# A joined set of edits in front of the state-space branch of a hybrid diffusion block, and two key units ahead of it

## The chip, the core and the metric

The kernel runs on one core of a Trainium2 chip. The metric is the device time of one execution in microseconds (us). The core has TensorE (PE in the profile; its weight loads are PEld), VectorE (DVE), ScalarE (ACT), GpSimd (POOL) and SyncE (SP), which here only issues DMAs. ACT issues DMAs as well, most of them stores. POOL issues a few.

## The reference, cut to what matters

One layer on 2048 latent tokens and 256 context tokens, width 1024. The input is normalised and modulated, projected once, and read by three branches: a 2-D Fourier mix, a bidirectional diagonal state-space scan (S5), and neighbourhood attention. The branches are gated, merged and projected; an MLP with squared ReLU follows.

```python
hx = modulate(rmsnorm(x, g_norm1[i]), sh1, sc1)
hc = modulate(rmsnorm(ctx, g_norm1[i]), mod_c[0], mod_c[1])
zx = hx @ w_in                       # 256 f | 256 u | 512 q | 512 k | 512 v | 3 x 1024 gates
zc_s5 = hc @ w_in[:, OFF_S5:OFF_Q]
zc_kv = hc @ w_in[:, OFF_K:OFF_G]
fa_x = fourier_mix(zx[..., :OFF_S5])
sb_x, sb_c = s5_branch(zx[..., OFF_S5:OFF_Q], zc_s5, ...)
nc_x = na_latent(qx, kx, vx, kc, vc, rpb)     # rpb: relative-position bias
out_x = gated_merge(fa_x, sb_x, nc_x, zx[..., OFF_G:], w_br_a, w_br_b, w_br_c, w_out)
x = x + gt1 * out_x
h2 = modulate(rmsnorm(x, g_norm2[i]), sh2, sc2)
x = x + gt2 * sqrelu_mlp(h2, w_ff1[i], w_ff2[i])
```

## The kernel before

Every product is made of three float32r products: each operand is split into a high part (rounded) and a low part (the rest), and `mm3` adds high by high, high by low and low by high (lines 179 to 181). A split is a copy on ACT for the high part and a subtraction on DVE or POOL for the low part (`splitw`, lines 169 to 175).

The projection is cut into units. A unit (`a_unit`, `gate`) takes 128 columns of `w_in`: `wunit` loads them on SP (tile `wraw`, two buffers, line 218), splits them into `whi` and `wlo` (two buffers each), and PE makes 24 products for each block of 512 tokens in PSUM tag `g`. ACT evicts to a tile `ev` (three buffers) and issues the store to DRAM. The kinds are f (Fourier), u (S5), q, k, v and gate. A q eviction also has a low part, made by DVE (line 325), and ACT issues the stores of both. The tokens are worked in two halves of 1024: `hx0`, then `hx1`, each 8 pairs of tiles.

A scheduler sets the order of the instructions on every engine and queue. It goes by readiness in its own model of time, and among ready instructions it takes the one that stands earlier in the program. Each engine and each queue then works strictly in that order. `issue_after(x)` puts DMAs behind x on their queue. Pools are stacks of memory, left and right; a pool opened after another was closed reuses its memory and waits for its last readers.

The order of the program: modulation and `hx0`; the S5 parameters (`s5_prep`, three steps, on DVE and POOL); u and f units of `hx0`; `hx1` (lines 392 to 396); the second part of the modulation weights, 64 loads `wm` of 256 KB on SP, each added by DVE (lines 400 to 430); the bias table (lines 433 to 447); the units of line 450 (k and v of `hx0`, u and f of `hx1`, q of `hx0`); S5; the late units of lines 467 to 469 (k, v, q of `hx1`, with `wlo` on POOL); the S5 gating; attention; 48 gate units; the merge and the MLP.

The bias table: `na_rpb` is transposed, mirrored by small copies on DVE and multiplied by a constant, giving `ro` of 120 x 128. Line 447 stores every row 64 times to `rpd` in DRAM, in pieces of 512 bytes. Attention reads it.

`hx0` is needed again for its gates, so `spill` stores it to DRAM, 1 MB for each of eight tile pairs. The Fourier stage's first table (`w1h`, `w1l`, 2 MB each) is copied from the constants to a DRAM tile `w1d` in eight transfers (line 461).

S5 (`s5`) has a drive (U, loaded by line 883, times L, loaded by line 899; lines 895 to 914), a scan on DVE alone (lines 945 to 978), and a readout. Its memory on the right side is that of `hx0`, so its loads begin when the last q unit of `hx0` is done. The Fourier branch (`fourier`) stands in the program between drive and scan. It has 16 table steps (line 532 on: load `zr` and the tables `fwh` and `fwl` from `w1d` on SP, products, copies to `ftA`). Then come `turn`, `tokens` and `channels`, whose PSUM results go through ACT twice, once as float32 (`Bf`, `Yf`) and once as the high part, and POOL subtracts (lines 561 and 578).

Of the kernel before, what the change touches and what calls it, by code (L numbers as in the profile page):

```python
# [94 lines left out]
def f32(t):  # L95
    return t.bitcast(F32)
# [3 lines left out]
def block_kernel(ctx: ExitStack, tc: tile.TileContext, I, out, C, stages=None, taps=None):  # L100
# [27 lines left out]
    gtd = dram.tile([2, D], F32, name="gtd")  # L128
    lmd = dram.tile([P, 512], F32, name="lmd")
    ld = dram.tile([8, P, 2, 256], F32, name="ld")  # L130
    w1d = dram.tile([2, P, 16, 256], F32, name="w1d")
    kmd = dram.tile([8, P, 256], F32, name="kmd")
    cd = dram.tile([8, P, 2, 2, P], F32, name="cd")
    x2d = dram.tile([2, KT, P, D], F32, name="x2d")
# [167 lines left out]
    def of_half(hx, half):  # L302
        return [(b * NB, NB, hx, half * HALF + b * NB) for b in range(2)]
# [54 lines left out]
    with pool("pa", side="right") as pa:  # L358
# [26 lines left out]
        for n in range(2):  # L385
            with tc.issue_after(lm):
                a_unit("u", n, of_half(hx0, 0) + [(0, CTX, hc, S)])
        next(prep5)
        next(prep5)
        for n in range(2):  # L390
            a_unit("f", n, of_half(hx0, 0))
        for _ in prep5:
            pass
        hst = ExitStack()
# [8 lines left out]
        for part in range(8):  # L403
# [16 lines left out]
            else:  # L420
# [7 lines left out]
                else:  # L428
                    nc.vector.tensor_tensor(a2[:, h], pt[:, 0:4], bm, op=OP.add)
                    nc.vector.scalar_tensor_tensor(a2[:, h], a2[:, h], 1.0, g2c[:, h], op0=OP.add, op1=OP.mult)  # L430


        rp = m2.tile([120, 31], F32, name="rp")
        nc.sync.dma_start(rp, I["na_rpb"].rearrange("l h a b -> (l h a) b"))
        pt = psum("t")
        nc.tensor.transpose(pt[0:31, 0:120], rp, ident[0:120, 0:120])
        rt = m2.tile([31, 8, 15], F32, name="rt")
        pv = pt[0:31, 0:120].rearrange("p (h a) -> p h a", h=8)
        for m in range(15):
            nc.vector.tensor_copy(rt[:, :, m], pv[:, :, 14 - m])  # L440
        rev = m2.tile([31, P], F32, name="rev")
        nc.sync.dma_start(rev, C["rev"])
        pt = psum("t")
        nc.tensor.matmul(pt[0:120, 0:P], rt.rearrange("p h a -> p (h a)"), rev, start=True, stop=True)
        ro = m2.tile([120, P], F32, name="ro")
        nc.vector.tensor_copy(ro, pt[0:120, 0:P])
        nc.sync.dma_start(rpd, ro[:, None, :].to_broadcast([120, 64, P]))
        m2s.close()

        for i, (kind, n) in enumerate([(c, n) for c in "kvufq" for n in range(2 if c in "uf" else 4)]):  # L450
            if kind in "uf":
                a_unit(kind, n, of_half(hx1, 1))
            else:
                a_unit(kind, n, of_half(hx0, 0) + ([] if kind == "q" else [(0, CTX, hc, S)]))
            with tc.issue_after(loads[-1]):
                if i < KT:
                    spill(hx0, i)
                elif i < 12:
                    r = slice((i % 4) * 32, (i % 4 + 1) * 32)
                    for e, nm in enumerate(("w1h", "w1l")):  # L460
                        nc.sync.dma_start(w1d[e, r], C[nm][r])

    g = K()
    g.__dict__.update(locals())
    if "s5" in stages:
        s5(g)
    for kind in "kvq":
        for n in range(4):
            a_unit(kind, n, of_half(hx1, 1), "pool")

    with pool("gl", side="right") as gl:
        wr = gl.tile([P, 2, 256], F32, name="wgr")
# [41 lines left out]
def fourier(g, ft):  # L514
# [13 lines left out]
    for ch in range(2):  # L528
        A = ft.tile([P, 2, 10, P], F32, name="ftA")
        for jj in range(8):  # L530
            zr = ft.tile([P, 2, P], F32, name="zr", bufs=2)
            nc.sync.dma_start(zr, zd[:, 2 * jj:2 * jj + 2, ch * P:(ch + 1) * P])
            zh = ft.tile([P, 2, P], F32R, name="zh", bufs=2)
            zl = ft.tile([P, 2, P], F32R, name="zl", bufs=2)
            g.splitw(zr, zh, zl)
            wh = ft.tile([P, 2, 256], F32R, name="fwh", bufs=2)
            wl = ft.tile([P, 2, 256], F32R, name="fwl", bufs=2)
            nc.sync.dma_start(f32(wh), g.w1d[0, :, 2 * jj:2 * jj + 2])
            nc.sync.dma_start(f32(wl), g.w1d[1, :, 2 * jj:2 * jj + 2])
            pt = psum("s")  # L540
            for j in range(2):
                mm3(pt[:, j * 256:(j + 1) * 256], zh[:, j], zl[:, j], wh[:, j], wl[:, j], True, True)
            for c in range(2):
                o = A[:, c].rearrange("p k (j i) -> p j k i", i=8)[:, 2 * jj:2 * jj + 2]
                i_ = pt.rearrange("p (j c k i) -> p c j k i", j=2, c=2, i=8)[:, c]
                for j in range(2):
                    nc.scalar.activation(o[:, j], i_[:, j, 0:10], AF.Copy)
# [3 lines left out]
        def turn(n):  # L551
# [3 lines left out]
            Bh = ft.tile([P, 2, 2, P], F32R, name="ftBh", bufs=2)  # L555
            Bl = ft.tile([P, 2, 2, P], F32R, name="ftBl", bufs=2)
            o = pt.rearrange("p (k c h) -> p k c h", k=2, c=2)
            Bf = ft.tile([P, 2, 2, P], F32, name="Bf")
            nc.scalar.activation(Bf, o, AF.Copy)
            nc.scalar.activation(Bh, o, AF.Copy)  # L560
            nc.gpsimd.tensor_tensor(Bl, Bf, f32(Bh), op=OP.subtract)
            B[n] = Bh, Bl

        def tokens(n):
# [7 lines left out]
            v = pt.rearrange("p (a c k) -> p a c k", a=2, c=2)  # L572
            Yh = ft.tile([P, 2, 2, P], F32R, name="Yh", bufs=2)
            Yl = ft.tile([P, 2, 2, P], F32R, name="Yl", bufs=2)
            Yf = ft.tile([P, 2, 2, P], F32, name="Yf")
            nc.scalar.activation(Yf, v, AF.Copy)
            nc.scalar.activation(Yh, v, AF.Copy)
            nc.gpsimd.tensor_tensor(Yl, Yf, f32(Yh), op=OP.subtract)
            Y[n] = Yh, Yl

        def channels(n):
# [1075 lines left out]
```

## Time and profile before

| what | us |
|---|---|
| median of 3 timed runs (lowest to highest) | 3142.71 (3140.58 to 3143.83) |
| the profiled execution | 3140.54 |
| its span, first to last instruction | 3138.8 |
| PE busy | 3007.0 (96%) |
| DVE busy | 2169.6 (69%) |
| ACT busy | 1422.8 (45%) |
| POOL busy | 940.5 (30%) |

All times inside the profile count from the first instruction of the span. "Busy" is the union of an engine's instructions. PE being busy does not mean that it is at full speed: the column PEclk gives the granted clock as a share of full. A name such as `ps_g<-hxh,whi` says what is written and what is read, without buffer numbers.

### The profile page before, as it was taken

Reading aid. Unit: us, or ns where it says so; the run is one execution under the profiler, and the core shown is the slowest. Engines: PE = TensorE matmul, PEld = TensorE weight load, DVE = VectorE, ACT = ScalarE, POOL = GpSimd, SP = SyncE. Lnnn points to the kernel's source line nnn. Section 1 sums busy time; section 2 is a strip of 40 time slices with the busy share of each in tenths; the row PEclk is TensorE's granted clock in tenths of the full one; section 3 lists DMA queues with packets and bytes.
Section 4 is the critical chain, followed back from the end, with each engine's and each line's share of the span. In section 5 each row is a group of like instructions: output and inputs, shape, how many; then the busy total and the mean of one; then the engine's idle time right before and its main releaser. Section 6 shows DMA issues by size and latency. Waiting matters only on the chain.

```text
span 3138.8 us, 40745 instructions
## 1 busy us (share of the span) xinstructions
PE 3007.0 (96%) x13974; PEld 2436.9 (78%) x13974; DVE 2169.6 (69%) x3654; ACT 1422.8 (45%) x2557; POOL 940.5 (30%) x865
## 2 busy tenths in 40 slices
PE   7999886899999999999999999999989999999998
PEld 4788675788788778887877788888867878878886
DVE  6534458984788888883748554777988475557788
ACT  4242143363566566653216555543432365555333
POOL 0520015301466655551511322311134022223111
PEclk9999988999999999999999999999999999999999
DMA  6669964456443633327533443845466334457442
GB/s 214 185 200 253 239 161 115 141 158 191 128 116 116 221 104 112 108 75 218 190 122 121 168 148 122 297 149 158 136 177 236 121 128 150 142 181 248 151 146 83
DMA packets 438213, 504.52 MB, mean 161 GB/s; under 512 B 95807, under 2 KB 281294, under 8 KB 437622
## 3 DMA queue, kind: packets, MB, share of 16 engines
q1 hardware_dynamic: 320646, 361.92, 38.2%
q10 hardware_dynamic: 116784, 139.09, 13.2%
q8 instruction: 110, 1.80, 0.2%
q0 software_dynamic: 576, 0.92, 0.1%
q14 instruction: 97, 0.79, 0.1%
HBM read 349.90 MB, written 156.11 MB: 161 GB/s over the span
## 4 chain that ended last, share of the span: by engine, by line
PE 65%; DVE 10%; DMA 5%; issue 1%; ACT 1%; SPq 1%; POOL 0%; ACTq 0%; DVEq 0%; POOLq 0%
PE ps_g L180 7%; PE ps_g L179 7%; PE ps_g L181 7%; PE ps_s L179 7%; PE ps_s L181 7%; PE ps_s L180 7%; PE ps_t L181 4%; PE ps_t L180 4%; PE ps_t L179 4%; PE ps_s L1110 3%; PE ps_o L1163 2%; PE ps_o L1162 2%; PE ps_o L1166 1%; DMA pgT<-rid 1%; DMA pgR<-in_w_out_dram 1%
## 5 line engine op out<-in xcount | busy, mean ns | idle before, releaser
L179 PE MATMUL ps_g<-hxh,whi 128*128 128x512 f32 x1024 | 407.1, 398 | 12.8 <-ACT ev L355 6.5
L180 PE MATMUL ps_g<-hxl,whi 128*128 128x512 f32 x1024 | 406.0, 396 | 0.0
L181 PE MATMUL ps_g<-hxh,wlo 128*128 128x512 f32 x1024 | 405.9, 397 | 0.0
L1160 POOL TENSOR_TENSOR pl<-st,ph 128x512 fp32r<-128x512 f32 (+7 forms) x256 | 270.4, 1071 | 165.6 <-ACT ph L1158 153.7
L1501 ACT ACTIVATE pgB<-pgB 128x1024 fp32r<-128x1024 f32 x112 | 118.8, 1061 | 303.6 <-PE ps_o L180 144.9
L179 PEld LDWEIGHTS ps_g<-hxh,whi 128*128 128x128 f32 x1024 | 195.0, 191 | 54.2 <-DVE ev L325 7.9
L180 PEld LDWEIGHTS ps_g<-hxl,whi 128*128 128x128 f32 x1024 | 195.0, 190 | 38.4 <-issue 0.5
L181 PEld LDWEIGHTS ps_g<-hxh,wlo 128*128 128x128 f32 x1024 | 195.1, 191 | 37.8
L1502 DVE TENSOR_TENSOR pgB<-pgB,pgB 128x1024 fp32r<-128x1024 f32 x112 | 148.5, 1327 | 89.0 <-ACT pgB L1501 88.9
L1353 DVE TENSOR_TENSOR pgW<-pgB,pgW 128x512 fp32r<-128x512 f32 x128 | 93.3, 733 | 142.3 <-ACT pgW L1352 142.3
L1132 DVE TENSOR_TENSOR mx<-mx,st 128x384 f32<-128x384 f32 (+2 forms) x224 | 184.5, 824 | 4.0
L180 PE MATMUL ps_s<-pgA,pgB 128*128 128x512 f32 x464 | 181.1, 390 | 0.0
L179 PE MATMUL ps_s<-pgA,pgB 128*128 128x512 f32 x464 | 181.1, 390 | 0.0
L181 PE MATMUL ps_s<-pgA,pgB 128*128 128x512 f32 x464 | 180.9, 390 | 0.0
L1390 POOL TENSOR_TENSOR pgR<-pgT 128x512 f32<-128x512 f32 x32 | 44.6, 1392 | 390.8 <-ACT pgT L1380 390.8
L1151 ACT ACTIVATE st<-st 128x512 f32<-128x512 f32 (+7 forms) x288 | 129.2, 494 | 66.2 <-DVE st L1150 56.6
L1537 POOL TENSOR_TENSOR pgA<-pgA,pgA 128x1024 f32<-128x1024 f32 x16 | 52.5, 3282 | 336.9 <-DMA pgA<-in_w_ff_dram 312.9
L1158 ACT ACTIVATE ph<-st 128x512 fp32r<-128x512 f32 (+7 forms) x288 | 135.7, 497 | 36.6 <-PE ps_o L1163 22.1
L180 PE MATMUL ps_g<-pgA,pgB 128*128 128x512 f32 x352 | 137.7, 391 | 1.3 <-DVE pgA L175 1.3
L179 PE MATMUL ps_g<-pgA,pgB 128*128 128x512 f32 x352 | 137.7, 391 | 0.0
L1150 DVE TENSOR_TENSOR st<-st,ps_t 128x512 f32<-128x512 f32 (+7 forms) x288 | 132.1, 524 | 8.1 <-PE ps_t L1142 8.0
L181 PE MATMUL ps_g<-pgA,pgB 128*128 128x512 f32 x352 | 137.5, 392 | 0.0
(506 smaller groups left out, 8418.9 us busy)
## 6 DMA issues: line engine op xcount, KB each, us to landing
pgB<-hcd SPq DMA_DIRECT2D x112, 512.0 KB
wraw<-in_w_in_dram SPq DMA_DIRECT2D x80, 512.0 KB
pgX<-in_w_ff_dram SPq DMA_DIRECT2D x64, 512.0 KB
hcd<-pgR ACTq DMA_DIRECT2D x64, 512.0 KB
pgA<-in_w_ff_dram SPq DMA_DIRECT2D x64, 512.0 KB
gd<-ev ACTq DMA_DIRECT2D x96, 256.0 KB
hcd<-pgT ACTq DMA_DIRECT2D x96, 256.0 KB
pgX<-gd SPq DMA_DIRECT2D x42, 512.0 KB
```

Of the source, the lines that this page charges most:

```text
L179: nc.tensor.matmul(out_, lh, rh, start=first, stop=False, skip_group_check=more)
L180: nc.tensor.matmul(out_, lh, rl, start=False, stop=False, skip_group_check=more)
L181: nc.tensor.matmul(out_, ll, rh, start=False, stop=last, skip_group_check=more)
L1110: nc.tensor.matmul(o, kk[:, j * P:(j + 1) * P], qs[:, i, p0:p1], start=i == 0, stop=i == 1)
L1132: v.tensor_tensor(M[:, c0:c1], M[:, c0:c1], st[:, c0:c1], op=OP.max)
L1150: v.tensor_tensor(st[:, c0:c1], st[:, c0:c1], mb[:, c0:c1], op=OP.subtract)
L1151: nc.scalar.activation(st[:, c0:c1], st[:, c0:c1], AF.Exp)
L1158: nc.scalar.activation(ph[:, c0:c1], st[:, c0:c1], AF.Copy)
L1160: e.tensor_tensor(pl[:, c0:c1], st[:, c0:c1], f32(ph)[:, c0:c1], op=OP.subtract)
L1353: v.tensor_tensor(p[:, 1], self.srcs[q][j], f32(p)[:, 0], op=OP.subtract)
L1501: nc.scalar.activation(h, s, AF.Copy)
L1502: v.tensor_tensor(l, s, f32(h), op=OP.subtract)
```

## The change

- The copy of the Fourier tables to `w1d` is gone. The Fourier steps read them from the constants, by DMAs that POOL issues into the float32r tiles.
- The spills: pairs 0 to 3 go out behind the loads of the two u units of `hx0`, pairs 4 to 7 behind the first four units of line 450.
- The bias table moves from the end of the second modulation part to the f units of `hx0`. It has a pool of its own. A further copy holds each row eight times, so that the store has pieces of 4 KB; it is cut in two, one behind each f unit's load.
- In `turn` and `tokens` ACT makes the high part alone, and DVE subtracts it from PSUM directly.
- The first two late units (k 0 and k 1 of `hx1`) stand ahead of S5 in the program, the other ten behind it as before. All twelve have `wlo` on DVE.

```diff
-    w1d = dram.tile([2, P, 16, 256], F32, name="w1d")
...
             with tc.issue_after(lm):
                 a_unit("u", n, of_half(hx0, 0) + [(0, CTX, hc, S)])
+            for k in range(2 * n, 2 * n + 2):
+                with tc.issue_after(loads[-1]):
+                    spill(hx0, k)
         next(prep5)
         next(prep5)
-        for n in range(2):
-            a_unit("f", n, of_half(hx0, 0))
+        with pool("rpp") as rpp:
...
+            ro = rpp.tile([120, P], F32, name="ro")
+            nc.vector.tensor_copy(ro, pt[0:120, 0:P])
+            ro8 = rpp.tile([120, 8, P], F32, name="ro8")
+            nc.vector.tensor_copy(ro8, ro[:, None, :].to_broadcast([120, 8, P]))
+            for n in range(2):
+                a_unit("f", n, of_half(hx0, 0))
+                with tc.issue_after(loads[-1]):
+                    r = slice(n * 60, (n + 1) * 60)
+                    nc.sync.dma_start(rpd[r].rearrange("r (a b) c -> r a (b c)", b=8),
+                                      ro8[r, None].rearrange("r a b c -> r a (b c)").to_broadcast([60, 8, 8 * P]))
...
-        rp = m2.tile([120, 31], F32, name="rp")
...
-        nc.sync.dma_start(rpd, ro[:, None, :].to_broadcast([120, 64, P]))
         m2s.close()
...
-            with tc.issue_after(loads[-1]):
-                if i < KT:
-                    spill(hx0, i)
-                elif i < 12:
-                    r = slice((i % 4) * 32, (i % 4 + 1) * 32)
-                    for e, nm in enumerate(("w1h", "w1l")):
-                        nc.sync.dma_start(w1d[e, r], C[nm][r])
+            if i < 4:
+                with tc.issue_after(loads[-1]):
+                    spill(hx0, 4 + i)
...
+    late = [(kind, n) for kind in "kvq" for n in range(4)]
+    for kind, n in late[:2]:
+        a_unit(kind, n, of_half(hx1, 1))
     if "s5" in stages:
         s5(g)
-    for kind in "kvq":
-        for n in range(4):
-            a_unit(kind, n, of_half(hx1, 1), "pool")
+    for kind, n in late[2:]:
+        a_unit(kind, n, of_half(hx1, 1))
...
-            nc.sync.dma_start(f32(wh), g.w1d[0, :, 2 * jj:2 * jj + 2])
-            nc.sync.dma_start(f32(wl), g.w1d[1, :, 2 * jj:2 * jj + 2])
+            nc.gpsimd.dma_start(wh, C["w1h"][:, 2 * jj:2 * jj + 2])
+            nc.gpsimd.dma_start(wl, C["w1l"][:, 2 * jj:2 * jj + 2])
...
-            Bf = ft.tile([P, 2, 2, P], F32, name="Bf")
-            nc.scalar.activation(Bf, o, AF.Copy)
             nc.scalar.activation(Bh, o, AF.Copy)
-            nc.gpsimd.tensor_tensor(Bl, Bf, f32(Bh), op=OP.subtract)
+            nc.vector.tensor_tensor(Bl, o, f32(Bh), op=OP.subtract)
...
-            Yf = ft.tile([P, 2, 2, P], F32, name="Yf")
-            nc.scalar.activation(Yf, v, AF.Copy)
             nc.scalar.activation(Yh, v, AF.Copy)
-            nc.gpsimd.tensor_tensor(Yl, Yf, f32(Yh), op=OP.subtract)
+            nc.vector.tensor_tensor(Yl, v, f32(Yh), op=OP.subtract)
```

## Rows read from the trace of the kernel before

**Rows 1.** The page's slices: busy tenths of PE, 40 slices of 78.5 us.
```profile
PE   7999886899999999999999999999989999999998
```
**Rows 2.** Windows: length, busy us (xinstructions) of each engine, PEclk, DMA share, GB/s.
```profile
356.00:659.00 303.00, 241.14 (x1195) 202.28 (x1194) 232.84 (x709) 105.95 (x251) 86.47 (x35) 0.89 0.56 146
...
600.00:656.00 56.00, 49.99 (x280) 42.90 (x279) 52.93 (x181) 24.15 (x51) 16.33 (x10) 1.00 0.33 97
...
800.00:1430.00 630.00, 627.03 (x3162) 502.55 (x3161) 527.21 (x945) 379.75 (x829) 364.75 (x502) 1.00 0.41 121
1430.00:1488.00 58.00, 55.19 (x235) 44.61 (x234) 15.71 (x20) 15.45 (x24) 0.00 (x0) 0.97 0.87 256
```
**Rows 3.** Timeline of PE: start, us, what, [idle before <-releaser].
```profile
393.33 0.61 PE L179 MATMUL ps_s<-Uh,Lh 128*128 128x288 f32 x1 [14.01 <-ACT Lh L171]
...
434.25 0.61 PE L179 MATMUL ps_s<-Uh,Lh 128*128 128x288 f32 x1 [10.31 <-ACT Lh L171]
...
504.37 0.55 PE L179 MATMUL ps_s<-fwh,zh 128*128 128x256 f32 x1 [15.00 <-DMA fwh<-w1d]
...
550.07 0.58 PE L179 MATMUL ps_s<-ft_w2h,ftBh 128*128 128x256 f32 x1 [7.19 <-ACT fa L595]
```
**Rows 4.** Timeline of SP's queue, 358 to 432 us.
```profile
360.54 5.21 SPq L883 DMA_DIRECT2D U<-ud  x5
...
371.32 5.82 SPq L408 DMA_DIRECT2D wm<-in_w_mod_dram  x3
...
384.14 0.90 SPq L899 DMA_DIRECT2D L<-ld  x2
...
405.11 1.01 SPq L447 DMA_DIRECT2D rpd<-ro  x1
406.64 24.05 SPq L899 DMA_DIRECT2D L<-ld  x2
```
**Rows 5.** Timeline of DVE in the drive.
```profile
433.00 0.26 DVE L970 COPY rev<-lam 128x16 f32<-128x16 f32 x2 [14.31 <-DMA rpd<-ro]
```
**Rows 6.** Timeline of POOL, 455 to 480 us.
```profile
455.51 0.75 POOL L522 DMA_DIRECT2D ft_w2h<-const_w2h_dram  x1 [9.08 <-DVE q L947]
...
459.86 2.46 POOL L175 TENSOR_TENSOR wlo<-wraw,whi 128x1024 fp32r<-128x1024 f32 x1 [2.00 <-ACT whi L171]
476.11 22.73 POOL L175 TENSOR_TENSOR wlo<-wraw,whi 128x1024 fp32r<-128x1024 f32 x1 [13.79 <-ACT whi L171]
```
**Rows 7.** Timeline of DVE at the same time.
```profile
460.02 2.58 DVE L175 TENSOR_TENSOR zl<-zr,zh 128x256 fp32r<-128x256 f32 x1
```
**Rows 8.** Groups of DVE, 450 to 655 us.
```profile
L325 DVE SCALAR_TENSOR_TENSOR ev<-ps_g,ev 128x512 fp32r<-128x512 f32 x8 | 5.4, 678 | 0.0
L175 DVE TENSOR_TENSOR wlo<-wraw,whi 128x1024 fp32r<-128x1024 f32 x4 | 4.9, 1221 | 1.8 <-ACT whi L171 1.8
```
**Rows 9.** Timeline of SP's queue, two neighbours in its order.
```profile
484.06 0.37 SPq L532 DMA_DIRECT2D zr<-zd  x1
498.87 0.38 SPq L218 DMA_DIRECT2D wraw<-in_w_in_dram  x1
```
**Rows 10.** Timeline of ACT in the Fourier stage.
```profile
549.36 0.65 ACT L595 ACTIVATE fa<-ps_s 128x256 f32<-128x256 f32 x1 [11.29 <-DVE q L947]
```
**Rows 11.** Windows in the first 300 us, columns as in rows 2.
```profile
60.00:80.00 20.00, 19.00 (x98) 13.99 (x96) 12.66 (x39) 11.12 (x23) 0.55 (x1) 1.00 0.13 29
...
235.00:300.00 65.00, 63.19 (x309) 52.03 (x308) 30.23 (x48) 14.04 (x24) 0.00 (x0) 1.00 0.97 264
```
**Rows 12.** Groups of POOL, 340 to 655 us: xcount | busy, mean ns | idle before.
```profile
L175 POOL TENSOR_TENSOR wlo<-wraw,whi 128x1024 fp32r<-128x1024 f32 x12 | 54.9, 4571 | 244.5 <-ACT whi L171 133.0 <-DMA wm<-in_w_mod_dram 111.4
L578 POOL TENSOR_TENSOR Yl<-Yf,Yh 128x512 fp32r<-128x512 f32 x10 | 16.9, 1692 | 17.5 <-ACT Yh L577 13.4 <-issue 4.1
```
**Rows 13.** Timeline of ACT: the high part of a gate unit's weights.
```profile
628.06 1.06 ACT L171 ACTIVATE whi<-wraw 128x1024 fp32r<-128x1024 f32 x1
```
**Rows 14.** Timeline of DVE: the low part of the same weights.
```profile
639.60 1.22 DVE L175 TENSOR_TENSOR wlo<-wraw,whi 128x1024 fp32r<-128x1024 f32 x1
```

More of the change, by code (lines that the diff above doesn't have):

```diff
@@ L387, in block_kernel @@
                 a_unit("u", n, of_half(hx0, 0) + [(0, CTX, hc, S)])
+            for k in range(2 * n, 2 * n + 2):
+                with tc.issue_after(loads[-1]):
+                    spill(hx0, k)
         next(prep5)
         next(prep5)
-        for n in range(2):
-            a_unit("f", n, of_half(hx0, 0))
+        with pool("rpp") as rpp:
+            rp = rpp.tile([120, 31], F32, name="rp")
+            nc.sync.dma_start(rp, I["na_rpb"].rearrange("l h a b -> (l h a) b"))
+            pt = psum("t")
+            nc.tensor.transpose(pt[0:31, 0:120], rp, ident[0:120, 0:120])
+            rt = rpp.tile([31, 8, 15], F32, name="rt")
+            pv = pt[0:31, 0:120].rearrange("p (h a) -> p h a", h=8)
+            for m in range(15):
+                nc.vector.tensor_copy(rt[:, :, m], pv[:, :, 14 - m])
+            rev = rpp.tile([31, P], F32, name="rev")
+            nc.sync.dma_start(rev, C["rev"])
+            pt = psum("t")
+            nc.tensor.matmul(pt[0:120, 0:P], rt.rearrange("p h a -> p (h a)"), rev, start=True, stop=True)
+            ro = rpp.tile([120, P], F32, name="ro")
[8 more added lines that the diff above has]
+                                      ro8[r, None].rearrange("r a b c -> r a (b c)").to_broadcast([60, 8, 8 * P]))
         for _ in prep5:
@@ L430, in block_kernel @@
                     nc.vector.scalar_tensor_tensor(a2[:, h], a2[:, h], 1.0, g2c[:, h], op0=OP.add, op1=OP.mult)
-        rp = m2.tile([120, 31], F32, name="rp")
[L434 to L446, printed above, removed]
-        nc.sync.dma_start(rpd, ro[:, None, :].to_broadcast([120, 64, P]))
         m2s.close()
```

## The prediction

> **What bounds the kernel now.** I read the page first, then windows by stage, then the waits inside the one stage that stands out. In the page's forty slices (78.5 us each) PE is at nine tenths or more but for the first, one near 2300 us, the last, and the fifth to the eighth, 314 to 628 us, where it falls to six [rows 1]. The windows say how much that is: from 356 to 659 us PE is busy 241.1 of 303 us, so 61.9 us are idle, and the granted clock averages 0.89; from 800 to 1430 us, attention with gate units as fill, PE is busy 627 of 630 [rows 2]. What the change can win lies in these 303 us: the start of the state-space branch, the Fourier branch and the scan on DVE. What it can lose lies anywhere.
>
> Four waits make 46.5 of the 61.9 us: 14.01 us before 393.33, 10.31 before 434.25, 15.00 before 504.37, 7.19 before 550.07 [rows 3]. The other 15.4 us are waits of at most a few us each.
>
> The first wait (A) ends with the split of the branch's first matrix. SP shows why it is late: the loads of U are issued from 360.5 on, but between them stand loads of the modulation weights (wm), and the load of L leaves only at 384.14 [rows 4].
>
> The second (B) is the bias table. Its store to rpd is issued at 405.11, and the next load on SP, the L that the drive needs, holds SP from 406.64 for 24.05 us [rows 4]. DVE stands too: a copy into a buffer that the store still reads starts at 433.00 after 14.31 us of idleness, released by that store [rows 5]. So one transfer stops two engines.
>
> The third (C) begins on POOL. A weight subtraction (wlo) that takes it 2.46 us at 459.86 takes 22.73 us at 476.11 [rows 6], amid the scan's back-to-back DVE instructions. The reverse happens too: at 460.02 DVE spends 2.58 us on a subtraction of 256 columns, while POOL's 2.46 us run [rows 7], though 1024 columns cost DVE 1.22 us otherwise [rows 8]. Both engines read two operands from SBUF, and they block each other. SP's next weight load waits for that wlo: nothing is issued between 484.06 and 498.87 [rows 9], and the Fourier tables queued behind it come late for PE at 504.37.
>
> The fourth (D) is ACT, held for 11.29 us in its own order until DVE, late against the order it was given, delivered a q eviction that ACT had to store [rows 10].
>
> **The change part by part.** *Bias table early, 4 KB rows.* The store leaves the drive. It no longer stands ahead of L on SP, and no scan buffer waits for it. B goes from 10.31 to between 0 and 3 us; I take 1, since the next L can still be late. What it costs at its new place: the small transposes and copies, one new copy of 120x1024 (nearest row 1.22 us on DVE [rows 8]) and the two stores, during the f units. SP is in order: if DVE delivers the copy late, the weight loads behind the store wait. I bound this by 0 and 6 us on PE and take 2.
>
> *Spills.* Eight pairs, 1 MB a pair, spread over the k and v units; now four pairs go out with the u units and four with the k units. From 60 to 80 us DMA is busy 0.13 [rows 11], so the first have room. Behind them on SP stand the weights of f: 0 to 4 us, I take 1.
>
> *The Fourier table's copy in DRAM goes.* Eight transfers of 512 KB leave SP; some of them lie in 235 to 300 us, where DMA is at 0.97 but PE is busy 63.2 of 65 us [rows 11]. So nothing comes directly. But the wm loads share SP and DMA with them, and wm is what delays L in A. I let A fall from 14.0 to between 3 and 14 us and take 7.
>
> *Two key units ahead of the branch.* PE already fills the time before A with late units; ahead in the order they can't come later, which protects A and gives nothing of its own: 0, bounds plus and minus 3.
>
> *wlo of the twelve late units, and Bl and Yl, from POOL to DVE.* POOL loses 54.9 us of wlo and 16.9 us of Yl [rows 12], as many Bl, and with them the blocked 22.73 us. DVE gains 12 x 1.22 = 14.6 us, and 20 subtractions that read PSUM, priced at the 0.68 us of the nearest row (128x512, one operand in PSUM), 13.6 us [rows 8]: 28 us in all. It gets back what POOL blocked: 12 x 2.46 + 20 x 1.69 = 63 us at most, nothing at least; DVE is busy 233 of 303 us [rows 2], so some three quarters of that fell on a busy DVE, and not all on an instruction with two SBUF operands. I take 25, under half. DVE's load is then about unchanged, and it is less late. ACT loses the 20 copies Bf and Yf, off the path. The new cover to watch: PSUM banks are held until DVE has read them.
>
> *Fourier tables from POOL's queue.* 32 loads leave SP, which no longer holds them behind a weight load. C's 15.0 us go to between 0 and 30 (the block twice over); I take 4. POOL's queue holds nothing else there. The trace has four such loads, issued from 455.51 amid the scan, 0.75 us for the first, and the POOL subtraction after them starts at 459.86 [rows 6]: they weren't stuck.
>
> By the Trainium skill, "SBUF — State Buffer", "SBUF: two separate sides", a DMA issued from GpSimd needs descriptors that GpSimd writes, and DVE in a two-port mode locks it out; "Who interferes with whom" adds that tensor_tensor takes only the read side, by inference. By the first sentence alone this edit walks into the trap that it means to leave; by the second it doesn't. The first row of [rows 6] fits the second. What the first would give is the second rival.
>
> *D and the small waits*, 7.2 and 15.4 us: many of them come from a late DVE. Between 5 and 23; I take 8.
>
> **The sum.** Idle in the stretch: 7 + 1 + 4 + 8 = 20 instead of 61.9, so 42 us. The clock: 0.89 over 303 us is about 67 us at the lower of its two levels (1.2 of 2.4 GHz), some half of it in the waits themselves; work at that level loses half its time, 2 to 33 us by how the two overlap, and I take 16. With a third of the idleness left, a third of this is left: 11 gained. The front costs 3. Total 42 + 11 - 3 = 50 us. A second way to the same: 241 us busy less 16 is 225 us of work at full clock; from 600 to 656 us, where gate units already have their wlo on DVE beside the scan, PE is busy 50.0 of 56 at clock 1.00 [rows 2]; 225 / 0.893 = 252 us, 51 less than 303.
>
> Does it reach the end? Behind this stretch PE is full, fed by gate units, and 58 us of gates alone follow attention [rows 2]. What is won earlier shortens that tail. The profiled execution took 3140.5 us (span 3138.8 and 1.7 around it), 2.2 under the median of 3142.7 and as fast as the fastest timed run. 3140.5 - 50 = 3090.5; on the median's footing 3093.
>
> **The rivals.** *DVE starves the weights (slower).* The late units' wlo now queues behind the scan. A gate unit's whi ends at 629.12 and its wlo starts on DVE at 639.60, 10.5 us later [rows 13, 14]; the q eviction of D was as late. With two buffers one unit's products cover it: 48 x 0.235 us (55.19 us for 235 products in the tail [rows 2]) = 11.3 us. Up to a lag of 10 us it is hidden; above, each of ten units pays the excess. The gain of 50 is gone at 5 us more each, a lag of 15; at 16 to 18 the time is 3093 + 60 to 80, so 3153 to 3173, with the upper part unlikely. For: DVE is busy 52.9 of 56 us from 600 to 656 us [rows 2]. Against: the same window, with gates' wlo on DVE, has PE at clock 1.00.
>
> *POOL's descriptors starve.* If the 32 loads are stuck in the scan's dense phases as wlo was for 20 us, PE pays a wait like C's 15 us once or twice: 3108 to 3123. For: the 22.73 us. Against: the four loads of [rows 6].
>
> *Given back.* The stretch shortens, but the gates taken forward are missing later: attention alone has DVE busy 527 of 630 [rows 2], and if the fill runs out before its end, or the loads behind attention lose the cover of the 58 us, up to all 50 come back: 3125 to 3148. It decides once the fill taken forward exceeds 58 us, which my sum does not.
>
> **How the numbers follow.** Forecast 0.60, 3093, own range 3064 (all waits and the slow clock gone, 79 us) to 3118. Starving descriptors 0.13. Given back 0.11. Starving weights 0.14. The other 0.02 is a front that costs tens of us. A change under 0.2% (6 us) is what a measurement of this kernel can't tell from none. Faster: 0.60 + 0.13 + 0.04 of the given back = 0.77. Same: 0.06 of the given back and 0.02 of a mild starving of weights, 0.08. Slower: the rest, 0.15. The range leaves out the starving weights and the top of the given back: 3064 to 3138.
>
> **What would show it.** B: no instruction on SP of more than a few us in the drive, no DVE idleness ended by rpd. C: no POOL subtraction in the Fourier stage, and first products of a table step not ended by its load. DVE: fewer instructions far above their group's usual length, and wlo starting within 10 us of whi. The tail of gates behind attention should be shorter or the whole should be earlier by the same amount. I am wrong if products of late units wait for wlo on DVE, if table loads land 15 us after their issue, or if the first 356 us grow by over 10.

## The result and the profile after

The changed kernel takes 3109.64 us (median of 4 runs, 3104.31 to 3111.11) against 3142.47 us (3140.58 to 3143.83) of the kernel before on the same chip: a ratio of 0.9893, 95% interval 0.9876 to 0.991. That is 33 us less, where 50 were forecast. The profiled execution took 3111.11 us, its span is 3109.3 us, against 3138.8 us before.

Where the 29.5 us between the two spans come from is read best from windows on either side of 375 us, just before the drive of the state-space branch. The columns are those of [rows 2]. First the kernel before:

```profile
0.00:375.00 375.00, 350.38 (x1754) 277.15 (x1755) 185.28 (x460) 122.68 (x215) 74.45 (x56) 0.97 0.75 218
375.00:700.00 325.00, 263.80 (x1350) 224.12 (x1349) 259.35 (x763) 133.38 (x307) 81.82 (x34) 0.89 0.55 150
```

and the changed kernel:

```profile
0.00:375.00 375.00, 334.65 (x1652) 263.94 (x1653) 189.05 (x478) 118.66 (x209) 66.34 (x53) 0.93 0.72 210
375.00:700.00 325.00, 308.15 (x1611) 263.48 (x1610) 263.47 (x799) 143.15 (x316) 19.40 (x36) 0.98 0.59 160
```

Two things happened. In the second stretch PE's idle time fell from 61.2 us (325 - 263.80) to 16.85, and the granted clock rose from 0.89 to 0.98. In the first, where the forecast put a cost of 3 us, the idle time rose from 24.6 to 40.4 us and the clock fell from 0.97 to 0.93.

For sums that take idle time and clock together I use one measure below, the **lost time** at a point of a trace: the time since the start less the time that the matmuls begun by then take without a stall (each shape at the 20th percentile of its distance to the next one, the same values for all kernels). Up to 375 us it went from 64.7 to 88.1 us, a loss of 23.4. From 375 to 700 us it went from 89.0 to 33.5 us, a gain of 55.5. Everything behind 700 us gave back 2.6 us. 55.5 - 23.4 - 2.6 = 29.5 us, the difference of the spans.

The waits of PE in the second stretch are short now (what waited, what it waited for: sum, times, longest):

```profile
PE ps_s L178 <- ACT Lh L170: 5.9, 1, 5.9
PE ps_g L178 <- DVE ev L324: 4.2, 4, 2.1
PE ps_s L180 <- DVE zl L174: 2.9, 2, 2.3
PE ps_s L180 <- DVE ftBl L565: 2.1, 1, 2.1
```

Of the four waits in [rows 3], A is 5.9 us long, and B, C and D are gone. In the first stretch a new one is longer than any of them. These are the timelines of PE, ACT and SP's queue around it, each with start, duration, instruction and the idle time before it (a row of several, such as x4, runs from the start of the first to the end of the last):

```profile
140.03 1.12 PE L334 MATMUL ps_o<-ident,ev 128*128 128x128 f32 x4 [16.05 <-ACT ev L331]
```
```profile
112.88 0.59 ACT L331 ACTIVATE ev<-ps_g 128x512 f32<-128x512 f32 x1
113.01 20.84 ACTq L340 DMA_DIRECT2D zd<-ev  x4
133.94 1.06 ACT L170 ACTIVATE whi<-wraw 128x1024 fp32r<-128x1024 f32 x1 [20.48 <-DMA zd<-ev]
```
```profile
107.20 1.96 SPq L415 DMA_DIRECT2D rpd<-ro  x2
109.26 2.46 SPq L217 DMA_DIRECT2D wraw<-in_w_in_dram  x1
111.77 13.23 SPq L271 DMA_DIRECT2D hxd<-hxah  x1
125.46 2.93 SPq L271 DMA_DIRECT2D hxd<-hxal  x1
```

SP issues the bias table's two stores (rpd) at 107.20 us, and behind them a weight load and two spills (hxd). ACT, which stores its own results on its own queue, stands at four small stores (zd) for 20.84 us from 113.01 on; other groups of four take 2.5 us (in the variant with the bias table left in place, below). While it stands there it splits no weights and evicts nothing, and PE stops.

It is not the issuing that takes so long. These are the four stores as a group (duration of one in ns, min/median/max), and the last three of them by themselves:

```profile
L340 ACTq DMA_DIRECT2D zd<-ev x4: 525/525/2447, 113.0 to 133.3; - x4
```
```profile
120.21 3.01 ACTq L340 DMA_DIRECT2D zd<-ev  x2
133.32 0.53 ACTq L340 DMA_DIRECT2D zd<-ev  x1
```

Between them ACT waits, and the semaphores in the trace (counters that a DMA raises as it lands) tell for what. The DMAs of SP and ACT are counted on the same eight semaphores, and a store of ACT first waits until the DMA before it on its semaphore has landed. ACT's second store comes behind the first bias store on its semaphore: that one has landed at 120.19 us, and ACT issues at 120.21. The fourth comes behind the second bias store: 133.30 and 133.32 us. Whether other semaphores would have freed PE was not run. It is not certain: the next weight load behind the bias stores on SP, issued at 109.26 us, has not landed before 135.06 either.

What the two queues moved in that time is in the DMA view from 107 to 134 us (q1 is SP's queue, q10 ACT's; packets, MB, share of the 16 DMA engines' time; then the issues with their size):

```profile
q1 hardware_dynamic: 2225, 5.27, 82.1%
q10 hardware_dynamic: 1005, 0.46, 6.2%
...
rpd<-ro SPq DMA_DIRECT2D x2, 1920.0 KB
```

SP's queue moved 5.27 MB, 3.93 of them the bias table (two stores of 1920 x 1024 bytes), ACT's 0.46 MB.

### The profile page after: what moved, and what is told of

The parts are those of the page before. It is cut to its first block, busy times and chain, and to the rows that moved or that the text cites. A ratio compares the mean times of both kernels' runs of the same rounds, so it can differ in the third digit from the quotient of the medians.

```text
span 3109.3 us, 40683 instructions
## 1 busy us (share of the span) xinstructions
PE 3004.7 (97%) x13974; PEld 2437.2 (78%) x13974; DVE 2168.5 (70%) x3687; ACT 1415.6 (46%) x2537; POOL 875.4 (28%) x865
## 3 DMA queue, kind: packets, MB, share of 16 engines
q1 hardware_dynamic: 309077, 349.33, 37.3%
## 4 chain that ended last, share of the span: by engine, by line
PE 73%; DVE 11%; DMA 7%; issue 1%; ACT 1%; SPq 1%; POOL 0%; ACTq 0%; DVEq 0%; POOLq 0%
PE ps_g L178 9%; PE ps_g L179 9%; PE ps_g L180 9%; PE ps_s L180 8%; PE ps_s L178 7%; PE ps_s L179 7%; PE ps_t L178 4%; PE ps_t L179 4%; PE ps_t L180 4%; PE ps_s L1112 3%; PE ps_o L1165 1%; PE ps_o L1164 1%; PE ps_o L1168 1%; DMA wm<-in_w_mod_dram 1%; DMA U<-ud 1%
## 5 line engine op out<-in xcount | busy, mean ns | idle before, releaser
L1162 POOL TENSOR_TENSOR pl<-st,ph 128x512 fp32r<-128x512 f32 (+7 forms) x256 | 276.8, 1095 | 166.1 <-ACT ph L1160 160.8
L174 DVE TENSOR_TENSOR wlo<-wraw,whi 128x1024 fp32r<-128x1024 f32 x80 | 109.7, 1371 | 84.3 <-ACT whi L170 84.3
L1153 ACT ACTIVATE st<-st 128x512 f32<-128x512 f32 (+7 forms) x288 | 129.8, 494 | 56.7 <-DVE st L1152 48.6
L1392 POOL TENSOR_TENSOR pgR<-pgT 128x512 f32<-128x512 f32 x32 | 44.3, 1384 | 392.5 <-ACT pgT L1382 392.5
L179 PE MATMUL ps_g<-pgA,pgB 128*128 128x512 f32 x352 | 137.7, 391 | 1.0 <-DVE pgA L174 1.0
L178 PE MATMUL ps_g<-pgA,pgB 128*128 128x512 f32 x352 | 137.7, 391 | 0.0
```

Of the source, the lines that this page charges most:

```text
L174: e.tensor_tensor(lo, raw, f32(hi), op=OP.subtract)
L178: nc.tensor.matmul(out_, lh, rh, start=first, stop=False, skip_group_check=more)
L179: nc.tensor.matmul(out_, lh, rl, start=False, stop=False, skip_group_check=more)
L1153: nc.scalar.activation(st[:, c0:c1], st[:, c0:c1], AF.Exp)
L1162: e.tensor_tensor(pl[:, c0:c1], st[:, c0:c1], f32(ph)[:, c0:c1], op=OP.subtract)
```

## The experiments

Three questions are open: which part of the change made the gain, what exactly makes the front slow, and whether the two parts can be had separately. The runs fell on other chips than the first pair; every ratio is to the kernel before on the same chip. All but one start from the changed kernel.

**The changed kernel once more**, as the yardstick for its neighbours.

> The changed kernel itself, beside the runs that follow, so that they are compared on the same chip. Both theories: ratio to the kernel before 0.989 (0.9876 to 0.991), the 16 us wait of TensorE near 140 us and a lost time (time minus the matmuls' own) of about 87 us at 350 us there again.

3104.32 us, ratio 0.9893 (0.9879 to 0.9908). The lost time at 375 us was 81.1 us here, 7 less than in the first profile, and 32.5 us from 375 to 700. So sizes in the front are good to some 7 us from one execution to the next, those of the second stretch to 1 us, as far as two profiles tell.

### What makes the front slow

**The bias table's stores behind the late units.**

```
-  # in the front, with the f units: prepare ro8, store it in two DMAs of 1.97 MB
+  # at the end of the second modulation part: prepare ro8
+  for i, (kind, n) in enumerate(late[2:]):
+      a_unit(kind, n, of_half(hx1, 1))
+      if i < 8:
+          with tc.issue_after(loads[-1]): <store 15 of the 120 rows, 0.49 MB>
```

> The bias table is prepared at the end of the second modulation part and stored in eight pieces behind eight of the ten late units, 2 KB rows; all else as in the changed kernel, which took 3109.6 us. Theory (the two early bias stores crowd ACT's stores out, and PE waits 16.05 us before 140.03): no wait over 5 us on PE between 100 and 200 us, the last hx0 product moves from 382.7 to 362 to 370, and the time is 3090 to 3098. Rival (the second four spills hold SP for 13 us at 111.77 and are the cause; the bias stores are bystanders): a wait of 10 us or more stays there, and the time is 3106 to 3112.

3090.01 us, ratio 0.986 (0.9845 to 0.9875). The 16 us wait is gone, and the lost time at 375 us is 65.4 us, that of the kernel before (64.7). The table's preparation moved along with its stores, but it is the stores whose landing ACT waited for, and they are therefore what made the front slow. But part of it came back: the stretch from 375 to 700 us lost 38.0 us, some 5 more than in the changed kernel, most of it in one wait (PE at 387.24 us, 10.50 us). ACT's timeline tells why it arises:

```profile
384.39 1.36 ACT L170 ACTIVATE Uh<-U 128x640 fp32r<-128x640 f32 x2 [18.45 <-DMA U<-ud]
...
386.61 0.58 ACT L318 ACTIVATE ev<-ps_g 128x512 f32<-128x512 f32 x1
```

In ACT's order the split of U stands ahead of the eviction (ev) of a key unit. ACT waits 18.45 us for U's load, the eviction queues behind it, and PE, which has a whole unit to do, has no free PSUM bank.

**The same stores in 512-byte pieces, at their new place.**

```
-  rpd[r] as rows of 8 x 128 <- ro8[r] (4 KB pieces)
+  nc.sync.dma_start(rpd[r], ro[r, None, :].to_broadcast([60, 64, P]))
```

> The two early bias stores are made of 512-byte pieces from the unreplicated row, as many bytes at the same place. Theory of piece size (4 KB pieces take turns with ACT's 512-byte pieces, so ACT gets an eighth of the bytes): ACT's stores of the f units take under 8 us for four instead of 20.84, PE's wait falls below 8 us, SP is held longer instead; 3098 to 3110. Rival (it is the bytes in the queues, whatever the pieces): the wait stays at 12 to 30 us; 3110 to 3125.

3101.18 us, ratio 0.9892 (0.9875 to 0.9908). The wait before 138.54 us is 15.63 us long:

```profile
PE ps_o L334 <- ACT ev L331: 19.7, 2, 15.6
```

The size of the pieces makes no difference here. The two bias stores have landed at 120.69 and 132.42 us, and ACT's stores behind them on their semaphores go out at 120.77 and 132.44: what counts is 3.93 MB in that place. The time in us lies in the range of the theory of piece size, but on this chip the kernel before was faster too (3136.34); the ratio is the changed kernel's, and that theory's short wait did not come.

**The second four spills behind the value units** instead of the key units; the first four stay with the u units.

```
-            if i < 4:
+            if 4 <= i < 8:
                 with tc.issue_after(loads[-1]):
-                    spill(hx0, 4 + i)
+                    spill(hx0, i)
```

> The second four spills go out behind the v units of hx0 instead of the k units; the bias stores stay early. Theory (bias stores): PE's wait before 140 stays at 10 us or more; 3104 to 3112. Rival (spills): the wait is gone; 3093 to 3099. If each carries half, the wait is 5 to 10 us and the time 3099 to 3105.

3098.54 us, ratio 0.9888 (0.9873 to 0.9902). The wait near 137 us shrinks only to 12.90, and the lost time at 375 us is 75.9 us:

```profile
PE ps_o L334 <- ACT ev L331: 12.9, 1, 12.9
```

The second bias store has landed at 132.83 us here, and ACT's store behind it goes out at 132.91. (The time in us is again in the rival's range, the ratio next to the changed kernel's.) The spills behind the bias table make the jam longer; they don't make it.

**The bias table back at its old place**, as it was, with all the rest of the change.

```
-  # in the front: prepare and store the bias table
+  # at the end of the second modulation part, as in the kernel before:
+  nc.sync.dma_start(rpd, ro[:, None, :].to_broadcast([120, 64, P]))
```

> Of the changed kernel, only the bias table goes back to where it was: prepared at the end of the second modulation part, stored in 512-byte pieces by one DMA ahead of the key units. Theory (the bias stores crowd out ACT's stores in the front): the wait of 16 us near 140 us is gone and the lost time at 350 us falls from 87 to 63 to 70 us; but the store again stands ahead of the loads for the drive, whose wait A is 12 to 15 us again instead of 5.9, and with it the stage loses 8 to 20 us: ratio 0.986 to 0.992, much the same. Rival: the spills alone make the front slow; then the wait near 140 us stays, lost time at 350 us stays over 80 us, and the ratio is 0.992 to 0.996.

3096.72 us, ratio 0.9871 (0.9855 to 0.9888), 7 to 8 us better than the changed kernel beside it, though the intervals overlap a little. At 375 us the lost time is 64.1 us, and four spills still run with the u units and four with the key units: on their own they cost nothing. ACT's timeline at the place of the jam:

```profile
109.61 2.50 ACTq L340 DMA_DIRECT2D zd<-ev  x4
...
115.93 2.49 ACTq L340 DMA_DIRECT2D zd<-ev  x4
```

From 375 to 700 us it lost 44.3 us instead of 32.5: the gain of moving the store out of the drive, 12 us, was smaller than the 17 us (81.1 - 64.1) that it cost in the front. The wait that is new against the changed kernel is the one before 385.85 us (11.96 us, an eviction behind U's split, as above); another, 5.96 us before 411.12, is as long as the changed kernel's A. The first has its like in the variant with late stores (10.50 us), so it is not shown to be the whole store's doing: in both kernels PE is at the drive some 20 us earlier, and U's loads are still to come.

### What made the gain in the scan

**The kernel before with the subtractions on DVE alone**, nothing else of the change.

```
-            a_unit(kind, n, of_half(hx1, 1), "pool")
+            a_unit(kind, n, of_half(hx1, 1))
...
-            nc.scalar.activation(Bf, o, AF.Copy)
             nc.scalar.activation(Bh, o, AF.Copy)
-            nc.gpsimd.tensor_tensor(Bl, Bf, f32(Bh), op=OP.subtract)
+            nc.vector.tensor_tensor(Bl, o, f32(Bh), op=OP.subtract)     # and Yl alike
```

> Of the kernel before, only the low halves of the late units' weights and of the Fourier steps move from POOL to DVE (with the two copies on ACT gone); units, tables, spills and bias table stay where they were. Theory: putting back the one or the other cost 18 and 24 us of the stage 375 to 700 us in the changed kernel, so this part alone brings 25 to 40 us: ratio 0.987 to 0.992, the stage loses 50 to 64 us instead of 89. Rival: the waits A (14 us) and C (15 us) for DMA set the scan's start and the table's steps and hide it; then 5 to 15 us, ratio 0.995 to 0.998.

3111.29 us, ratio 0.9914 (0.9896 to 0.9931): 27 of the change's 33 us from two of its seven edits. The stretch from 375 to 700 us loses 48.6 us instead of 89.0. PE's waits from 100 to 700 us show what is left and what isn't:

```profile
PE ps_s L179 <- ACT Lh L171: 21.9, 2, 11.7
PE ps_g L179 <- ACT ev L319: 2.7, 1, 2.7
PE ps_s L181 <- DVE zl L175: 2.5, 1, 2.5
```

A and B are still there (11.67 and 10.23 us), as nothing was done about them. C is gone, although the tables still come by SP's queue behind the weights. Of the 40 us won up to 700 us, 11 came back between 700 and 1500 us (55.3 us lost against 43.8), some 5 of them from 750 to 800 us and 5 from 1000 to 1100; why stays open.

**The late weights' subtraction back on POOL.**

```
-        a_unit(kind, n, of_half(hx1, 1))
+        a_unit(kind, n, of_half(hx1, 1), "pool")     # all twelve late units
```

> The low parts of the twelve late units' weights are again made by POOL; all else as in the changed kernel. Theory (POOL and DVE block each other on operands in SBUF): at least one POOL subtraction over 10 us in the scan, the scan's DVE instructions sum to 195 us or more instead of 188, 3114 to 3130. Rival (POOL's blocking cost time only because SP had the table loads behind a weight load): wlo may be blocked, but PE waits less than 6 us more in all and the time is 3106 to 3113.

3123.79 us, ratio 0.9962 (0.9949 to 0.9975). The stretch loses 50.7 us, 17 to 18 more. POOL's timeline, and the wait of PE that follows:

```profile
458.76 25.09 POOL L174 TENSOR_TENSOR wlo<-wraw,whi 128x1024 fp32r<-128x1024 f32 x1 [3.54 <-ACT whi L170]
483.80 0.58 POOL L545 DMA_DIRECT2D fwl<-const_w1l_dram  x1
484.37 0.55 POOL L544 DMA_DIRECT2D fwh<-const_w1h_dram  x1
...
485.96 2.39 POOL L174 TENSOR_TENSOR wlo<-wraw,whi 128x1024 fp32r<-128x1024 f32 x1
```
```profile
489.97 0.58 PE L178 MATMUL ps_s<-fwh,zh 128*128 128x256 f32 x1 [18.21 <-DMA fwh<-const_w1h_dram]
```

One subtraction stands 25.09 us where its neighbour takes 2.39 (of the other eleven, eight take 2.4 us and three 3.2 to 6.6), and the table loads behind it on POOL's queue wait with it. This is [rows 6] again, one queue further.

**The Fourier steps' subtractions back on POOL** (with the copies that feed them), the late weights on DVE.

```
+            nc.scalar.activation(Bf, o, AF.Copy)
             nc.scalar.activation(Bh, o, AF.Copy)
-            nc.vector.tensor_tensor(Bl, o, f32(Bh), op=OP.subtract)
+            nc.gpsimd.tensor_tensor(Bl, Bf, f32(Bh), op=OP.subtract)    # and Yl alike
```

> Of the changed kernel, the low halves of the Fourier steps go back to POOL, with the two additional copies on ACT; all else stays. Theory: what delayed POOL before was the low halves of the weights that blocked it (22.73 us in one of them); with those gone from POOL its subtraction comes in time, DVE sheds some 25 us in a stage where it is full, and the stage 375 to 700 us gets shorter by 0 to 10 us: ratio 0.986 to 0.989. Rival: POOL is held up by DVE in each of the subtractions for themselves as it was in the split of the weights; then TensorE waits for POOL near 520 to 600 us, 10 to 20 us in all, ratio 0.992 to 0.996.

3129.74 us, ratio 0.9973 (0.9964 to 0.9982). I had expected this to be harmless or a little better, and by the trace it was the dearest edit of all: 24 us more are lost from 375 to 700 us (56.5). With no weights left on POOL, one of its own short subtractions is stuck:

```profile
537.23 1.56 POOL L584 TENSOR_TENSOR Yl<-Yf,Yh 128x512 fp32r<-128x512 f32 x1 [1.41 <-issue]
545.93 10.42 POOL L584 TENSOR_TENSOR Yl<-Yf,Yh 128x512 fp32r<-128x512 f32 x1 [7.14 <-ACT Yh L583]
```

and PE waits for it before 556.41 us (10.17 us), and for a DVE eviction before 530.43 us (7.42). So it isn't the weights alone. A short subtraction on POOL can be caught too, though only one of the twenty was for long; the others took 1.3 to 2.8 us. It works in both directions, as one group of the scan's instructions shows (L960 before, L962 in the changed kernel, L966 here: the same 68 additions of 128x8 on DVE; durations min/median/max in ns). Before:

```profile
L960 DVE TENSOR_TENSOR Sx<-Sx,q x68: 158/170/1253, 499.0 to 619.8; 128x8 f32<-128x8 f32 x68
```

after:

```profile
L962 DVE TENSOR_TENSOR Sx<-Sx,q x68: 163/169/176, 496.0 to 604.6; 128x8 f32<-128x8 f32 x68
```

and in this variant:

```profile
L966 DVE TENSOR_TENSOR Sx<-Sx,q x68: 157/170/1291, 493.6 to 612.5; 128x8 f32<-128x8 f32 x68
```

The medians are equal; only the longest, some 1.1 us above the median, come and go with POOL's work.

**The tables by SP again**, with their copy in DRAM.

```
-            nc.gpsimd.dma_start(wh, C["w1h"][:, 2 * jj:2 * jj + 2])
+            nc.sync.dma_start(f32(wh), g.w1d[0, :, 2 * jj:2 * jj + 2])   # wl alike
+            elif 8 <= i < 12:      # behind the u units: copy w1h, w1l to w1d
```

> Of the changed kernel, the copy of the table w1 into the chip's own memory comes back, and SP loads the two halves of each step from it, as before; all else stays. Theory (the prediction's term C, 15 us down to 4): the table's loads queue behind SP's loads of weights for the late units, TensorE waits 8 to 15 us more in the table's steps (466 to 580 us), ratio 0.992 to 0.995. Rival: wait C came from the bias table's stores ahead of it, which are gone from this stretch anyway; then the ratio stays at 0.988 to 0.991, no wait over 5 us in those steps, and moving the loads to POOL's queue was worth nothing.

3108.47 us, ratio 0.9907 (0.9893 to 0.9922), 4 us above its neighbour, with intervals that overlap. PE's waits in the trace:

```profile
PE ps_t L443 <- DVE acc L438: 13.8, 1, 13.8
...
PE ps_s L179 <- DMA fwh<-w1d: 3.1, 4, 1.2
```

C doesn't come back: four waits for the tables, 3.1 us together. What comes is a wait of 13.8 us at 407.95 us for the modulation sums, whose weights (wm) now share SP with the copies; A is gone then, so it takes A's place more than it adds to it (37.3 us lost from 375 to 700, 4.8 more).

### The two units and a better kernel

**The two key units behind the branch again.**

```
-    for kind, n in late[:2]:
-        a_unit(kind, n, of_half(hx1, 1))
     if "s5" in stages:
         s5(g)
-    for kind, n in late[2:]:
+    for kind, n in late:
```

> Of the changed kernel, the two key units go back behind the state-space branch; all else stays. Theory (term A of the prediction): ahead of the drive they are TensorE's work while U and L come in; without them the stretch 375 to 425 us loses 18 to 25 us instead of 10, ratio 0.991 to 0.994. Rival: the drive is bound by the transfers of U and L themselves, which the two units' own loads and stores only push back; then the ratio stays at 0.988 to 0.991.

3112.25 us, ratio 0.9917 (0.99 to 0.9935): at the theory's edge and overlapping the changed kernel's. Wait A is 9.53 us instead of 5.92, but from 375 to 425 us 12.8 us are lost, not the theory's 18 to 25, and the stretch from 375 to 700 us loses 34.8 us instead of 32.5 to 33.5. So the units are worth 1 to 4 us by the traces; the rest of the 7.5 us between the ratios is within what the runs can't tell.

**Three units ahead**, in the variant with the late bias stores (`late[:3]`, `late[3:]`).

> The variant with the bias table's stores behind the late units, with three units instead of two ahead of the state-space branch. Theory: the wait of 10.5 us that came up near 387 us is for U's loads, and one more unit of some 12 us covers it: the stretch 375 to 425 us loses 3 to 7 us instead of 13, ratio 0.982 to 0.984. Rival: the DMA engines are full from 355 to 410 us, the third unit's loads and stores push U and L back by as much, and the ratio stays at 0.985 to 0.988.

3103.96 us, ratio 0.9896 (0.9875 to 0.9917): a miss, by the ratios 11 us worse than with two. The wait that it was meant to cover is still there, 12.27 us before 386.70 us, for the reason given above: it isn't work that PE lacks but a bank, and ACT, which would free one, stands at U's split for 19.46 us.

```profile
383.86 0.74 ACT L170 ACTIVATE Uh<-U 128x640 fp32r<-128x640 f32 x1 [19.46 <-DMA L<-ld]
...
386.07 0.58 ACT L318 ACTIVATE ev<-ps_g 128x512 f32<-128x512 f32 x1
```

Two more waits came up behind it, 4.14 us before 456.74 and 3.87 before 554.12 us. Neither theory had named ACT's order.

**Late bias stores and the second four spills behind the value units, together.**

> The variant with the bias table's stores behind the late units, and with it the second four spills behind the value units. Theory (the spills crowd out ACT's stores in the front for themselves): 3 to 6 us better than with the late bias stores alone, ratio 0.984 to 0.985. Rival: with the bias stores gone from the front the spills find room there (lost time at 375 us was 64 to 65 us with them, 64.7 before); then 0.9855 to 0.987, no better.

3086.52 us (3082.28 to 3089.6), ratio 0.9836 (0.9817 to 0.9855): the fastest, 52 us under the kernel before and some 18 under the changed one. The lost time at 150 us is 37.8 us, 4.7 under the variant with the bias stores moved alone, and at 375 us 64.1 against 65.4. Whether the spills' new place is worth 3 us more is not settled; the intervals of the two overlap.

| Variant | ratio | lost to 375 us | lost 375 to 700 us |
|---|---|---|---|
| before | 1 | 64.7 | 89.0 |
| changed kernel (first profile; second) | 0.9893 | 88.1; 81.1 | 33.5; 32.5 |
| bias stores behind late units | 0.986 | 65.4 | 38.0 |
| bias stores in 512-byte pieces | 0.9892 | 86.3 | 33.0 |
| second spills behind value units | 0.9888 | 75.9 | 35.5 |
| bias table at its old place | 0.9871 | 64.1 | 44.3 |
| before, subtractions on DVE | 0.9914 | 64.1 | 48.6 |
| late weights on POOL | 0.9962 | 84.9 | 50.7 |
| Fourier steps on POOL | 0.9973 | 85.8 | 56.5 |
| tables by SP | 0.9907 | 78.1 | 37.3 |
| two units behind the branch | 0.9917 | 83.8 | 34.8 |
| three units ahead, late bias stores | 0.9896 | 64.1 | 43.9 |
| late bias stores, late spills | 0.9836 | 64.1 | 35.7 |

## Why the prediction was right, and where it was not

**The stage was sized right.** The forecast for the stretch (there 356 to 659 us) was 42 us of idle time and 11 us of clock. Measured from 375 to 700 us: 44.4 us of idle time (61.2 - 16.85), and 55.5 - 44.4 = 11.1 us of clock. The single waits came out near their terms: A 5.9 (7), B 0 (1), C 0 (4), D and the small waits 11.0 (8). That the sum agrees is in part luck, as the credit for it was put on other edits than those that earned it (below).

**The front was mis-sized.** The step is the one on the bias table at its new place. It put 2 us (0 to 6) on the transposes, copies and stores and 1 us on the spills; the two together cost 23.4 us between the two profiles, 17 to 20 us of it the bias table. That share is the lost time at 375 us that goes away with its stores, against a kernel with the changed front on the same chip: 81.1 - 64.1 = 17.0 beside the changed kernel, 84.9 - 65.4 = 19.5 beside the variant with the late weights on POOL. I had looked for what queues behind the stores on SP and for how late DVE delivers, and not at which other engine must wait until they have landed. The row was there: behind the very same store SP's loads of L were held up for 24.05 us in the kernel before [rows 4]. Moved, the 3.93 MB took about as long to land, 26.1 us (107.20 to 133.30) against 27.8 (405.11 to 432.91), and what waited for it now was ACT's queue. The text named its own test, "if the first 356 us grow by over 10", and that is what happened. With the front at 23 instead of 3 its sum gives 30 us, and the two spans differ by 29.5.

**The credit was partly put on the wrong edit.** The table loads were given 11 us for C. The chain in the first part of the prediction (POOL's subtraction stuck, SP's weight load behind it, the tables behind that) was right, and cutting its first link is enough: C is gone in the kernel before with the subtractions on DVE alone, and doesn't return when the tables go back to SP. The move of the bias table was given B's 9 us; in fact the stretch loses 12 us less with it, and it costs more than that in front. A's 7 us were put on the copies that leave SP; with the copies back, A is gone all the same, and the stretch loses 4.8 us more by another wait. The two units ahead were put at 0, bounds plus and minus 3; 1 to 4 us were seen. Taken alone the two edits with DVE bring 27 us, and all the others together the remaining 6, which the overlapping intervals can't tell from none.

**DVE bore the load.** It was to gain 28 us and to get 25 back. Over the whole span its busy time is 2168.5 us against 2169.6 before, with some 28 us of work added, so it got back a little more than that. (From 375 to 700 us it rose from 259.35 to 263.47 us, but the changed kernel has 36 more DVE instructions in that window.) The 20 short subtractions take 680 and 676 ns each (0.68 was taken):

```profile
L565 DVE TENSOR_TENSOR ftBl<-ps_t,ftBh 128x512 fp32r<-128x512 f32 x10 | 6.8, 680 | 0.0
L580 DVE TENSOR_TENSOR Yl<-ps_s,Yh 128x512 fp32r<-128x512 f32 x10 | 6.8, 676 | 0.0
```

**Starved weights did not occur.** That rival needed a lag of 15 us between the high and the low half. The longest in the scan is 8.1 us, from the end of the one at 474.99 us to the start of the other:

```profile
473.93 1.06 ACT L170 ACTIVATE whi<-wraw 128x1024 fp32r<-128x1024 f32 x1 [2.95 <-PE ps_g L179]
```
```profile
483.11 1.25 DVE L174 TENSOR_TENSOR wlo<-wraw,whi 128x1024 fp32r<-128x1024 f32 x1
```

**Starved descriptors did not occur.** The sixteen loads of the tables' high halves, issued from POOL while DVE runs the scan, take 537 ns each to issue and land in time (from issue to landing, min/median/max):

```profile
L544 POOL DMA_DIRECT2D fwh<-const_w1h_dram x16: 537/537/540, 457.8 to 571.2; - x16
...
DMA to landing us min/median/max: 3.4/4.6/7.2
```

Of the two readings of the Trainium skill that the prediction weighed ("SBUF — State Buffer", "Who interferes with whom"), the one holds by which tensor_tensor on two SBUF operands disturbs GpSimd's reads but not its descriptors: single subtractions of POOL got stuck for 10 to 25 us beside these instructions, while none of the 32 loads of the tables took more than 0.54 us to issue.

**Little was given back.** Behind 700 us the changed kernel lost 2.6 us more than before. In the variant with the subtractions on DVE alone 11 us were given back; whether by the way that this rival names is not shown.

## What to carry to other kernels

A transfer that is moved takes its bytes along: before it goes to a place with "room on the queue", add up how long it takes to land there, look which instructions of other engines wait for that, on their own data or on a shared semaphore, and spread it in pieces over work that stores little. Two engines that block each other at their operands were best parted altogether here; leaving only the short instructions on the second engine cost 24 us of the stage. And when a change of many edits is right in sum, run its parts: here two of them made four fifths of the gain, and one of the rest had a negative sign.

## What the runs showed of the hardware

**A bulk transfer on one queue can hold another engine's queue.** ACT's four stores of 64 KB stood for 20.84 us while SP's 3.93 MB and the spills ran, 2.5 us otherwise. No single issue took over 2.45 us; the two long pauses ended 0.02 us after the two bias stores had landed, whose semaphores ACT's next stores use. With pieces of 512 bytes it was 0.08 and 0.02 us, and PE's wait 15.63 us against 16.05 with 4 KB. Small stores also land later beside the bulk: the one issued at 113.01 us took 10.7 us, one at 105.90, ahead of it, 2.0. By the Trainium skill ("DMA: Bandwidth & Descriptors", "Queues, rings and completion order") a DMA engine takes turns between its queues packet by packet; no run here tests that, as ACT's queue was held at the semaphores for most of the time.

**A blocked POOL instruction can wait through a whole run of DVE's.** The 25.09 us of one subtraction on POOL are ten times its neighbour's 2.39, and in these 25 us 73 DVE instructions start; a DVE instruction that is caught pays, in the group shown, some 1.1 us (1291 against 170 ns). Here DVE, which issued back to back, went on and POOL stood; what decides between them no run shows.

**The clock follows the wait.** From 110 to 140 us, with the 16 us wait in it, the granted clock averages 0.80, against 0.94 before in the same window. From 130 to 145 us it is 0.50, the lower of its two levels, so the first 5 us of products behind the wait, which ends at 140.03, run at the lower level as well.
